# High and low rows side by side: one 512-column product in place of two of 256 columns, with the PSUM halves added afterwards

## The chip, the cores and the metric

The kernel runs on one core of a Trainium2 chip. The metric is the device time of one execution in microseconds (us). Every run is one launch with the same inputs.

## The reference

One layer of a hybrid diffusion backbone, batch 1, 256 latent tokens and 256 context tokens, model width 2048, float32. Two token mixers run in parallel, an RWKV-7 scan (branch a) and a gated DeltaNet (branch b). The change lies behind them, where the branches are merged, projected, and put through the feed-forward part:

```python
def gated_merge(o_a, o_b, gate_cols, p_a, p_b, w_out):
    g_a, g_b = jnp.split(gate_cols, 2, axis=-1)
    m = jax.nn.sigmoid(g_a) * (o_a @ p_a) + jax.nn.sigmoid(g_b) * (o_b @ p_b)
    return m @ w_out

def swiglu(h, w_gate_up, w_down):
    gate, up = jnp.split(h @ w_gate_up, 2, axis=-1)
    return (jax.nn.silu(gate) * up) @ w_down
...
        x = x + gt1 * y
        x = x + gt2 * swiglu(modulate(rmsnorm(x, norm2_w[layer]), sh2, sc2),
                             ffn_w_gate_up[layer], ffn_w_down[layer])
    return rmsnorm(x, final_norm_w)
```

`o_a` and `o_b` are 256 x 1024, `p_a` and `p_b` 1024 x 2048, `w_out` 2048 x 2048, gate and up together 2048 x 11264, down 5632 x 2048. The six modulation rows (`sh1` to `gt2`) come from one more product, of the condition vector with a 2048 x 12288 matrix.

## The kernel before

Everything is stored with channels on the 128 partitions and the 256 tokens along the free dimension (`T = 256`). A product with a weight matrix makes one tile of 128 output channels at a time and runs over the input channels in steps of 128 (`k`). Accuracy comes from a split into two numbers of the type float32r, one that TensorE takes in a single pass: a value is a high part (the value cast) plus a low part (the value less the high part). A step is then three products into the same 256 columns of a PSUM bank, in `gemm` (L376):

```python
E.matmul(ps, hi, Xh[:, k, :n], start=first and i == 0, stop=False)
E.matmul(ps, hi, Xl[:, k, :n], start=False, stop=False)
E.matmul(ps, lo, Xh[:, k, :n], start=False, stop=last and i == len(wt) - 1)
```

The weights arrive as float32 and are split on the chip, in `load_w`: a piece of eight steps (128 x 1024 numbers) is loaded into `wraw` on the SyncE queue, ScalarE casts it into `whi` (L370), VectorE subtracts into `wlo` (L371), and TensorE uses both. There are three buffers of `wraw` and two each of `whi` and `wlo` (four from the ninth tile of the first merge half to the end of the output projection). A cast can begin when TensorE has done with the piece that holds the buffer.

The stages behind the mixers, each a loop over output tiles `j`:

- First merge half: 16 tiles of 8 steps with the rows `Oa` (`oah`, `oal`), each multiplied by its sigmoid gate out of PSUM (L1589) into `PA`.
- Second merge half: 16 tiles of 8 steps with the rows of branch b in the same `Oa`, multiplied by the gate (L1609), added to `PA` (L1610), and split into the rows `M` (`mh`, `ml`).
- Output projection: 16 tiles of 16 steps with `M`. VectorE adds each, scaled, to the stream `x1` (L1623), ScalarE squares it, VectorE sums the squares (L1626). In these three loops VectorE also accumulates two modulation rows, the shift and scale of the feed-forward part, from a matrix that the GpSimd queue loads in 32 pieces: 31 steps on `acc` (L1565), one at each start of a row (L1567). For each row, four small matmuls sum over partitions, and a copy (`arow`, L1552), two transposes and two adds (L1557) bring it into `mod`. The tiles' first weights for gate and up (`w4`) are split in the same loop.
- Seam: sum of the squares by two pairs of matmuls with ones (L401), logarithm and exponential on ScalarE, and normalisation into the rows `Hf` (`hfh`, `hfl`, L1654 to L1656). It needs `x1` in full and `mod`.
- Gate and up: 44 pairs of tiles with 16 steps each. Gate and up share a bank, 256 columns each. ScalarE makes the SiLU out of PSUM (L1676), VectorE multiplies it with the up half out of PSUM (L1677), and the result is split into `Z` (`za` for the first 32 tiles, `zb` for the rest; L385, L386). The first two pairs use `w4`. In 32 of the tiles the last modulation row is made beside it (`aw`, L1688).
- Down: 16 tiles of 44 steps with `Z`, added to `x1` (L1701) as in the projection; then the last norm and the store.

The order of each engine's instructions in these stages is set when the program is built: a scheduler sorts what the code emits by its own estimate of times. Only what is wrapped in `tc.keep_in_program_order` keeps its place. On the chip each engine takes its instructions in that order. `pst` takes a PSUM bank from a pool: `pmm` has three (tile name `mm`), `psq` two (`s`).

Of the kernel before, what the change touches and what calls it, by code (L numbers as in the profile page):

```python
# [18 lines left out]
P = 128  # L19
D = 2048  # L20
KT = D // P
T = 256
# [261 lines left out]
def emit(ctx: ExitStack, tc, A, out, dbg=None):  # L284
# [91 lines left out]
    def gemm(ps, wt, X, n, first=True, last=True):  # L376

        Xh, Xl = X
        for i, (k, hi, lo) in enumerate(wt):
            E.matmul(ps, hi, Xh[:, k, :n], start=first and i == 0, stop=False)  # L380
            E.matmul(ps, hi, Xl[:, k, :n], start=False, stop=False)  # L381
            E.matmul(ps, lo, Xh[:, k, :n], start=False, stop=last and i == len(wt) - 1)  # L382

# [1193 lines left out]
    Oa = (gp.tile([P, 8, T], F32R, name="oah"), gp.tile([P, 8, T], F32R, name="oal"))  # L1577
    for i in range(0, 8, 2):
        split(Oa[0][:, i:i + 2, :], Oa[1][:, i:i + 2, :], rows[:, i:i + 2, :])
# [3 lines left out]
    for j in range(KT):  # L1583
# [16 lines left out]
    for i in range(0, 8, 2):  # L1600
        split(Oa[0][:, i:i + 2, :], Oa[1][:, i:i + 2, :], ob[:, i:i + 2, :])
    m_ctx = ExitStack()
    mp = m_ctx.enter_context(tc.tile_pool(name="mp", bufs=1, reuse_waits="tile"))
    M = (mp.tile([P, KT, T], F32R, name="mh"), mp.tile([P, KT, T], F32R, name="ml"))
    for j in range(KT):
        ps = pst(pmm, "mm")
        gemm(ps[:, 0:T], load_w(A["pb"][j], P, 8), Oa, T)
        m = x1p.tile([P, T], F32, tag="m", name="m")
        V.tensor_mul(m, ps[:, 0:T], gts[:, 16 + j])  # L1609
        V.tensor_add(m, m, PA[:, j])  # L1610
        split(M[0][:, j], M[1][:, j], m)
# [36 lines left out]
    with tc.tile_pool(name="fp", bufs=1, reuse_waits="tile") as fp:  # L1648
        Hf = (fp.tile([P, KT, T], F32R, name="hfh"), fp.tile([P, KT, T], F32R, name="hfl"))
        s2 = x1p.tile([P, 16], F32, name="s2")  # L1650
        V.scalar_tensor_tensor(s2, mod[:, 64:80], 1.0, p_("n2"), ALU.add, ALU.mult)
        for k in range(KT):
            hb = x1p.tile([P, T], F32, tag="hb", name="hb")
            V.scalar_tensor_tensor(hb, x1[:, k, :], s2[:, k:k + 1], r, ALU.mult, ALU.mult)  # L1654
            S.activation(Hf[0][:, k, :], hb, AF.Identity, bias=mod[:, 48 + k:49 + k])
            V.scalar_tensor_tensor(Hf[1][:, k, :], hb, mod[:, 48 + k:49 + k], Hf[0][:, k, :].bitcast(F32),  # L1656
                                   ALU.add, ALU.subtract)
        p4 = [pst(pmm, "mm") for _ in range(2)]
        for k in range(KT):
            for a in range(4):  # L1660

                gemm(p4[a // 2][:, T * (a % 2):T * (a % 2) + T], w4[a][k:k + 1], Hf, T,
                     k == 0 and a % 2 == 0, k == KT - 1 and a % 2 == 1)
        Z = (zap.tile([P, 2, 32, T], F32R, tag="za", name="za"), fp.tile([P, 2, NH - 32, T], F32R, name="zb"))
# [3 lines left out]
        for j in range(NH):  # L1668
            if j < 2:
                ps = p4[j]  # L1670
# [135 lines left out]
```

## Time and profile before

| what | value |
|---|---|
| median of 3 runs | 2228.19 us (2222.93 to 2228.29) |
| the profiled execution | 2235.21 us, its span 2233.3 us |
| granted TensorE clock, mean over the span | 0.983 |
| TensorE matmuls busy | 2158.9 us, 97% |
| VectorE, ScalarE busy | 1554.9 us (70%), 1062.6 us (48%) |
| first product of the merge, of gate and up, of down, from the span's start | 1268.9, 1470.9 and 1968.9 us |

How the lines are read: `L382 PE MATMUL mm<-hfh,wlo` is line 382, on TensorE, writing the tile `mm` from `hfh` and `wlo`. PE is TensorE's matmuls, PEld its weight loads, DVE is VectorE, ACT ScalarE, POOL GpSimd, SP SyncE. In groups, `x1344 | 376.3, 280 | 0.0` means 1344 instructions, 376.3 us busy, 280 ns each, and 0.0 us in which the engine sat idle before them, followed by who ended that wait. In a timeline a row is start, duration, engine, line and operation; `[1.52 <-PE mm L381]` is an idle time before it and what ended it. A table of windows has, per stretch of time, the busy time of each engine with its instructions, then the granted clock, the share of the DMA engines and GB/s.

### The profile page before, as it was taken

The page shows a single profiled execution, that of the slowest core. Times are in us where ns is not written, and L with a number is a line of the kernel's source. Part 1 is how long each engine was busy: PE and PEld are TensorE (multiplying, and loading weights), DVE is VectorE, ACT ScalarE, POOL GpSimd, SP SyncE. Part 2 cuts the span into 40 slices and gives each one's busy share as a digit, 9 for nine tenths or more (in the row PEclk, how much of TensorE's full clock was granted, in tenths as well). Part 3 has the DMA queues.
Part 4 walks back from the last instruction along what each step waited for, and adds up shares of the span by engine and source line. Part 5 has one row for each costly group of instructions (what it writes and reads, how often), then busy time and mean ns, then how long its engine had stood idle before and what let it go on. Part 6 is the DMA issues. An engine that isn't in the chain of part 4 may idle for free.

```text
span 2233.3 us, 54391 instructions
## 1 busy us (share of the span) xinstructions
PE 2158.9 (97%) x22780; PEld 1929.1 (86%) x22780; DVE 1554.9 (70%) x3244; ACT 1062.6 (48%) x1872; POOL 95.0 (4%) x171
## 2 busy tenths in 40 slices
PE   6998999999999999999999999999999999999998
PEld 4776687777778788878789999999999999999997
DVE  3457487788888668898998788955666565444444
ACT  3256545444554555544455555544444444444443
POOL 0000000000000011011110010100000000000000
PEclk9999899999999999999999999999999999999999
DMA  9975544344343446555567798937777776566665
GB/s 382 414 193 172 158 116 121 97 115 108 97 123 109 113 139 196 161 177 180 172 196 254 263 345 271 350 102 231 232 233 228 236 234 198 187 183 185 182 183 158
DMA packets 234484, 435.13 MB, mean 195 GB/s; under 512 B 115328, under 2 KB 129664, under 8 KB 229888
## 3 DMA queue, kind: packets, MB, share of 16 engines
q1 hardware_dynamic: 206304, 355.11, 50.6%
q0 software_dynamic: 14112, 51.39, 7.1%
q10 hardware_dynamic: 13824, 25.17, 3.4%
q8 instruction: 178, 2.92, 0.5%
q14 instruction: 66, 0.54, 0.1%
HBM read 405.76 MB, written 25.84 MB: 193 GB/s over the span
## 4 chain that ended last, share of the span: by engine, by line
PE 45%; issue 39%; DVE 9%; DMA 4%; ACT 2%; POOL 0%; SPq 0%; POOLq 0%; ACTq 0%; DVEq 0%
PE mm L147 22%; PE s L147 6%; PE pa L147 4%; DVE arena L147 3%; PE pi L147 3%; PE mm L380 3%; PE mm L382 2%; PE mm L381 2%; DVE wlo L147 2%; PE mm L477 1%; DVE aw L147 1%; DMA wraw<-w_low 1%; DMA aw<-ada_rest 1%; DMA ct<-ctxT 0%; DVE LAl L147 0%
## 5 line engine op out<-in xcount | busy, mean ns | idle before, releaser
L371 DVE TENSOR_TENSOR wlo<-wraw,whi 128x1024 fp32r<-128x1024 f32 x328 | 392.7, 1198 | 327.0 <-ACT whi L370 324.0
L370 ACT CAST whi<-wraw 128x1024 fp32r<-128x1024 f32 x328 | 336.6, 1028 | 467.7 <-PE mm L381 408.7
L147 PE MATMUL mm<-hxh,whi 128*128 128x256 f32 (+1 forms) x1376 | 466.1, 339 | 4.1 <-ACT whi L147 2.4
L147 PE MATMUL mm<-hxh,wlo 128*128 128x256 f32 (+1 forms) x1376 | 463.8, 337 | 5.0 <-DVE wlo L147 4.7
L147 PE MATMUL mm<-hxl,whi 128*128 128x256 f32 (+1 forms) x1376 | 463.3, 337 | 0.7 <-issue 0.7
L382 PE MATMUL mm<-hfh,wlo 128*128 128x256 f32 x1344 | 376.3, 280 | 0.0
L380 PE MATMUL mm<-hfh,whi 128*128 128x256 f32 x1344 | 375.1, 279 | 0.0
L381 PE MATMUL mm<-hfl,whi 128*128 128x256 f32 x1344 | 375.0, 279 | 0.0
L147 PEld LDWEIGHTS mm<-hxh,wlo 128*128 128x128 f32 x1376 | 265.1, 193 | 31.1 <-DVE wlo L147 7.8
L147 PEld LDWEIGHTS mm<-hxh,whi 128*128 128x128 f32 x1376 | 264.8, 192 | 28.2 <-ACT whi L147 3.2
L147 PEld LDWEIGHTS mm<-hxl,whi 128*128 128x128 f32 x1376 | 264.5, 192 | 23.5 <-issue 4.0
L147 DVE TENSOR_TENSOR wlo<-wraw,whi 128x512 fp32r<-128x512 f32 x344 | 236.9, 690 | 49.6 <-ACT whi L147 48.4
L381 PEld LDWEIGHTS mm<-hfl,whi 128*128 128x128 f32 x1344 | 252.5, 188 | 0.0
L382 PEld LDWEIGHTS mm<-hfh,wlo 128*128 128x128 f32 x1344 | 252.3, 188 | 0.2 <-DVE wlo L371 0.2
L380 PEld LDWEIGHTS mm<-hfh,whi 128*128 128x128 f32 x1344 | 251.4, 187 | 0.0
L147 ACT CAST whi<-wraw 128x512 fp32r<-128x512 f32 x344 | 205.5, 617 | 83.1 <-PE mm L147 57.3
L147 DVE TENSOR_TENSOR arena<-arena 128x28 f32<-128x28 f32 (+13 forms) x538 | 131.4, 246 | 23.0 <-DMA arena<-scr 10.0
L380 PE MATMUL mm<-za,whi 128*128 128x256 f32 x512 | 145.1, 283 | 0.0
L382 PE MATMUL mm<-za,wlo 128*128 128x256 f32 x512 | 145.0, 283 | 0.0
L381 PE MATMUL mm<-za,whi 128*128 128x256 f32 x512 | 144.9, 283 | 0.0
L147 ACT ACTIVATE arena<-arena 128x512 f32<-128x512 f32 (+3 forms) x132 | 76.6, 593 | 45.6 <-DVE arena L147 33.8
L380 PEld LDWEIGHTS mm<-za,whi 128*128 128x128 f32 x512 | 98.2, 192 | 0.0
(325 smaller groups left out, 3897.9 us busy)
## 6 DMA issues: line engine op xcount, KB each, us to landing
wraw<-w SPq DMA_DIRECT2D x172, 512.0 KB, 4.1
wraw<-wgu SPq DMA_DIRECT2D x168, 512.0 KB, 4.7
aw<-ada_rest POOLq DMA_DIRECT2D x96, 512.0 KB, 5.3
aw<-ada_first SPq DMA_DIRECT2D x32, 1024.0 KB, 12.6
wraw<-wdn SPq DMA_DIRECT2D x64, 448.0 KB, 3.5
wraw<-wout SPq DMA_DIRECT2D x32, 512.0 KB, 6.6
aw<-ada_gt ACTq DMA_DIRECT2D x64, 256.0 KB, 4.8
wraw<-wdn SPq DMA_DIRECT2D x32, 512.0 KB, 3.6
```

The lines of the kernel that those rows point to most:

```text
L147: return Op(self, cost, lambda: getattr(self.engine, name)(out, *a, **k), kind)
L370: S.copy(hi[:, c, :M], raw[:, c, :M])
L371: V.tensor_sub(lo[:, c, :M], raw[:, c, :M], hi[:, c, :M].bitcast(F32))
L380: E.matmul(ps, hi, Xh[:, k, :n], start=first and i == 0, stop=False)
L381: E.matmul(ps, hi, Xl[:, k, :n], start=False, stop=False)
L382: E.matmul(ps, lo, Xh[:, k, :n], start=False, stop=last and i == len(wt) - 1)
L477: E.matmul(ps[32 * g:32 * g + 32, 0:P], ckr[:, k].rearrange("p a b -> p (a b)"), aws[e, c][:, i, g], start=k == 0, stop=k == KT - 1)
```

## The change

The high and low rows of an operand become one tile with the two beside each other for every step (`[P, k, 2, T]`). In `gemm_wide` the high weights go once through both, 512 columns, and fill a whole bank: high times high in the left half, high times low in the right. The low weights go through the high rows and add to the right half. A step has two products in place of three, and the same 768 columns. The halves are added afterwards: `both` copies the right one with ScalarE and adds the left one with VectorE; where the result goes into `x1`, the update is made twice, once from each half. Gate and up take a bank each, up from the pool `psq`.

```diff
+    def gemm_wide(ps, wt, X, first=True, last=True):
+        for i, (k, hi, lo) in enumerate(wt):
+            E.matmul(ps, hi, X[:, k].rearrange("p a t -> p (a t)"), start=first and i == 0, stop=False)
+            E.matmul(ps[:, T:512], lo, X[:, k, 0], start=False, stop=last and i == len(wt) - 1)
+
+    def both(out, ps):
+        S.copy(out, ps[:, T:512])
+        V.tensor_add(out, ps[:, 0:T], out)
...
-    Oa = (gp.tile([P, 8, T], F32R, name="oah"), gp.tile([P, 8, T], F32R, name="oal"))
+    Oa = gp.tile([P, 8, 2, T], F32R, name="oa")
...
-        gemm(ps[:, 0:T], load_w(A["pa"][j], P, 8), Oa, T)
+        gemm_wide(ps, load_w(A["pa"][j], P, 8), Oa)
...
-        V.tensor_mul(PA[:, j], ps[:, 0:T], gts[:, j])
+        both(PA[:, j], ps)
+        V.tensor_mul(PA[:, j], PA[:, j], gts[:, j])
...
-        V.tensor_mul(m, ps[:, 0:T], gts[:, 16 + j])
+        both(m, ps)
+        V.tensor_mul(m, m, gts[:, 16 + j])
...
-        gemm(ps[:, 0:T], load_w(A["wout"][j], P, KT), M, T)
-        V.scalar_tensor_tensor(x1[:, j, :], ps[:, 0:T], mod[:, 32 + j:33 + j], x1[:, j, :], ALU.mult, ALU.add)
+        gemm_wide(ps, load_w(A["wout"][j], P, KT), M)
+        for part in (ps[:, T:512], ps[:, 0:T]):
+            V.scalar_tensor_tensor(x1[:, j, :], part, mod[:, 32 + j:33 + j], x1[:, j, :], ALU.mult, ALU.add)
...
-        p4 = [pst(pmm, "mm") for _ in range(2)]
+        p4 = [pst(pmm, "mm") if a % 2 == 0 else pst(psq, "s") for a in range(4)]
...
-                ps = pst(pmm, "mm")
-                gemm(ps[:, 0:T], load_w(A["wgu"][2 * j], P, KT), Hf, T)
-                gemm(ps[:, T:512], load_w(A["wgu"][2 * j + 1], P, KT), Hf, T)
+                pg, pu = pst(pmm, "mm"), pst(psq, "s")
+                gemm_wide(pg, load_w(A["wgu"][2 * j], P, KT), Hf)
+                gemm_wide(pu, load_w(A["wgu"][2 * j + 1], P, KT), Hf)
             g = fp.tile([P, T], F32, tag="g", name="g", bufs=2)
-            S.activation(g, ps[:, 0:T], AF.Silu)
-            V.tensor_mul(g, ps[:, T:512], g)
+            u = fp.tile([P, T], F32, tag="u", name="u", bufs=2)
+            both(g, pg)
+            S.activation(g, g, AF.Silu)
+            both(u, pu)
+            V.tensor_mul(g, u, g)
...
-                gemm(ps[:, 0:T], [(k - 32 * i, hi, lo) for k, hi, lo in wt if k // 32 == i],
-                     (z[:, 0], z[:, 1]), T, i == 0, i == 1)
-            V.scalar_tensor_tensor(x1[:, j, :], ps[:, 0:T], mod[:, 80 + j:81 + j], x1[:, j, :], ALU.mult, ALU.add)
+                gemm_wide(ps, [(k - 32 * i, hi, lo) for k, hi, lo in wt if k // 32 == i], z, i == 0, i == 1)
+            for part in (ps[:, T:512], ps[:, 0:T]):
+                V.scalar_tensor_tensor(x1[:, j, :], part, mod[:, 80 + j:81 + j], x1[:, j, :], ALU.mult, ALU.add)
```

The scheduler sorts the new instructions in, and moves others. Two places matter below. A line number of the changed kernel is 10 to 14 higher than before: the update L1623 is now L1636, L1565 (`acc`) L1575, L1552 (`arow`) L1562, L1557 (`mod`) L1567, L1626 (sum of squares) L1639.

VectorE at the end of the output projection, before the change. `arena<-mm` is the update of `x1` by an output tile, `acc` a step of a modulation row, `arow` and `mod` its end; the last update belongs to the last tile:

```order
L1565 SCALAR_TENSOR_TENSOR acc<-aw,ck,acc 128x1024
L1623 SCALAR_TENSOR_TENSOR arena<-mm,mod,arena 128x256
L371 TENSOR_TENSOR wlo<-wraw,whi 128x1024 x2
L1626 TENSOR_TENSOR arena<-arena 128x256
L371 TENSOR_TENSOR wlo<-wraw,whi 128x1024
L1552 COPY arow<-pa 128x256
L1623 SCALAR_TENSOR_TENSOR arena<-mm,mod,arena 128x256
L371 TENSOR_TENSOR wlo<-wraw,whi 128x1024
L1626 TENSOR_TENSOR arena<-arena 128x256
L1557 TENSOR_TENSOR mod<-pa,PR 128x4 x2
L1651 SCALAR_TENSOR_TENSOR arena<-mod,PR 128x16
L1623 SCALAR_TENSOR_TENSOR arena<-mm,mod,arena 128x256
```

The same end after the change:

```order
L371 TENSOR_TENSOR wlo<-wraw,whi 128x1024
L1575 SCALAR_TENSOR_TENSOR acc<-aw,ck,acc 128x1024
L1639 TENSOR_TENSOR arena<-arena 128x256
L1636 SCALAR_TENSOR_TENSOR arena<-mm,mod,arena 128x256 x2
L1575 SCALAR_TENSOR_TENSOR acc<-aw,ck,acc 128x1024
L1636 SCALAR_TENSOR_TENSOR arena<-mm,mod,arena 128x256
L1639 TENSOR_TENSOR arena<-arena 128x256
L1575 SCALAR_TENSOR_TENSOR acc<-aw,ck,acc 128x1024
L1562 COPY arow<-pa 128x256
L1567 TENSOR_TENSOR mod<-pa,PR 128x4 x2
L1664 SCALAR_TENSOR_TENSOR arena<-mod,PR 128x16
```

The last two steps of `acc` and the end of the row, which stood ahead of the last tile's update, now stand behind its first half; the second half stands between the two steps.

ScalarE in one pair of tiles of gate and up, before the change (`g<-mm` is the SiLU, `za<-g` the split's cast, `aw` a load that ScalarE's queue issues):

```order
L370 CAST whi<-wraw 128x1024 x2
L1676 ACTIVATE g<-mm 128x256
L370 CAST whi<-wraw 128x1024
L385 CAST za<-g 128x256
L370 CAST whi<-wraw 128x1024
L1687 DMA aw<-ada_gt 128x512 x2
```

And after it:

```order
L370 CAST whi<-wraw 128x1024
L391 COPY g<-mm 128x256
L1701 DMA aw<-ada_gt 128x512 x2
L370 CAST whi<-wraw 128x1024
L1689 ACTIVATE g<-g 128x256
L370 CAST whi<-wraw 128x1024
L391 COPY u<-s 128x256
L370 CAST whi<-wraw 128x1024
L395 CAST za<-g 128x256
```

Every one of the four casts of weights now has another instruction of ScalarE behind it, two of them copies out of PSUM, and the SiLU reads what VectorE has added (L392) in place of the bank.

More of the change, by code (lines that the diff above doesn't have):

```diff
@@ L1576, in emit @@
     PA = gp.tile([P, KT, T], F32, name="PA")
[L1577 removed]
+    Oa = gp.tile([P, 8, 2, T], F32R, name="oa")
     for i in range(0, 8, 2):
[L1579 removed]
+        split(Oa[:, i:i + 2, 0], Oa[:, i:i + 2, 1], rows[:, i:i + 2, :])
     gts = gp.tile([P, 32, T], F32, name="gts")
@@ L1648, in emit @@
     with tc.tile_pool(name="fp", bufs=1, reuse_waits="tile") as fp:
-        Hf = (fp.tile([P, KT, T], F32R, name="hfh"), fp.tile([P, KT, T], F32R, name="hfl"))
+        Hf = fp.tile([P, KT, 2, T], F32R, name="hf")
         s2 = x1p.tile([P, 16], F32, name="s2")
```

21 lines of the change are left out of this document (10 added, 11 removed).

## The prediction

> **What bounds the kernel now.** I read the head of the page first, then the costliest groups.
>
> ```profile
> span 2233.3 us, 54391 instructions
> PE 2158.9 (97%) x22780; PEld 1929.1 (86%) x22780; DVE 1554.9 (70%) x3244; ACT 1062.6 (48%) x1872; POOL 95.0 (4%) x171
> L371 DVE TENSOR_TENSOR wlo<-wraw,whi 128x1024 fp32r<-128x1024 f32 x328 | 392.7, 1198 | 327.0 <-ACT whi L370 324.0
> L370 ACT CAST whi<-wraw 128x1024 fp32r<-128x1024 f32 x328 | 336.6, 1028 | 467.7 <-PE mm L381 408.7
> L382 PE MATMUL mm<-hfh,wlo 128*128 128x256 f32 x1344 | 376.3, 280 | 0.0
> ```
>
> TensorE sits at 97%, and the wait columns run in a circle that ends there: the subtraction on VectorE (L371) waits for the cast on ScalarE (L370), and the cast waits for TensorE to give a weight buffer back. The products (L382) wait for nothing. That is the whole kernel, though, and the change touches only its last 950 us, so I asked for the stages of that stretch: end of the first merge half, second half, output projection, the seam before the feed-forward part, gate and up, down.
>
> ```profile
> core 0: us, PE busy (x) PEld busy (x) DVE busy (x) ACT busy (x) POOL busy (x), PEclk, DMA share, GB/s
> 1305.00:1328.00 23.00, 22.87 (x192) 22.86 (x192) 22.78 (x27) 15.97 (x21) 3.73 (x7) 1.00 0.98 357
> 1328.00:1374.00 46.00, 45.62 (x384) 45.43 (x383) 42.72 (x70) 22.73 (x32) 2.65 (x5) 1.00 0.79 279
> 1374.00:1467.00 93.00, 92.96 (x792) 91.50 (x791) 81.13 (x100) 47.20 (x57) 8.51 (x16) 1.00 0.90 317
> 1494.00:1969.00 475.00, 475.00 (x4033) 474.83 (x4032) 273.05 (x384) 202.32 (x255) 0.00 (x0) 1.00 0.69 218
> 1969.00:2222.00 253.00, 252.75 (x2115) 252.49 (x2113) 120.88 (x127) 107.05 (x128) 0.00 (x0) 1.00 0.61 178
> ```
>
> In the last two rows TensorE alone is full and VectorE idles for nearly half the time. In the first three VectorE is as full as TensorE: 22.78 of 23, 42.72 of 46, 81.13 of 93 us. A shorter product is therefore worth something in gate, up and down, and an added VectorE instruction costs something in the merge.
>
> **What a product costs.** A matmul's busy time (280 ns) overlaps the next one, so the price is the distance between starts. From the window rows it is 475.00 / 4033 = 117.8 ns in gate and up, and 252.75 / 2115 = 119.5 ns in down. A 512-column product of this kind occurs in the input projection, which the change leaves alone. The first and last starts of an undisturbed run of each width there:
>
> ```profile
> 825.63 0.39 PE L147 MATMUL mm<-hxh,whi 128*128 128x512 f32 x1
> ...
> 831.98 0.39 PE L147 MATMUL mm<-hxl,whi 128*128 128x512 f32 x1
> 1207.14 0.28 PE L147 MATMUL mm<-hxh,whi 128*128 128x256 f32 x1
> ...
> 1210.73 0.28 PE L147 MATMUL mm<-hxh,whi 128*128 128x256 f32 x1
> ```
>
> 28 steps in 6.35 us make 226.8 ns at 512 columns, 30 steps in 3.59 us make 119.7 at 256. The slope is 107.1 / 256 = 0.418 ns a column, and 12.6 ns are left that each instruction costs whatever its width. The changed group does the same columns (512 + 256 instead of three times 256) in one instruction fewer, so it saves that fixed part. With 107.1 ns of columns, the fixed part is 117.8 - 107.1 = 10.7 ns in gate and up, and 119.5 - 107.1 = 12.4 in down.
>
> - Gate and up: 88 tiles x 16 = 1408 steps x 10.7 ns = 15.1 us less.
> - Down: 16 tiles x 44 = 704 steps x 12.4 ns = 8.7 us less. Together 23.8.
>
> What no row shows is 512 and 256 columns in turn, all the time. Rows at a switch bound it, once up and once down, and so does a run of 512 just after an interruption:
>
> ```profile
> 841.49 0.28 PE L147 MATMUL mm<-hxh,wlo 128*128 128x256 f32 x1
> 841.61 0.40 PE L147 MATMUL mm<-hxh,whi 128*128 128x512 f32 x1
> 841.84 0.40 PE L147 MATMUL mm<-hxl,whi 128*128 128x512 f32 x1
> 852.29 0.39 PE L147 MATMUL mm<-hxh,wlo 128*128 128x512 f32 x1
> 852.52 0.28 PE L147 MATMUL mm<-hxh,whi 128*128 128x256 f32 x1
> 852.63 0.28 PE L147 MATMUL mm<-hxl,whi 128*128 128x256 f32 x1
> 766.09 0.40 PE L147 MATMUL mm<-hxh,wlo 128*128 128x512 f32 x1
> ...
> 768.18 0.39 PE L147 MATMUL mm<-hxh,wlo 128*128 128x512 f32 x1
> ```
>
> A pair takes 0.35 us at the first switch and 0.34 at the second. The disturbed run makes 9 steps in 2.09 us, 232 ns each, and so a pair of 352. Against three times 119.7 = 359 that saves from 7 to 19 ns a step. The undisturbed rows give 226.8 + 119.7 = 346.5, inside these ends, and I take them because gate, up and down run undisturbed. The ends move the 23.8 us to 12.0 (5.6 ns less on each of 2112 steps) and to 37.3 (6.4 ns more).
>
> The Trainium skill ("TensorE: Matmul & The Clock Gate", section "Back-to-back issue gap") puts the fixed part at about 2.5 ns. By that the two stages would save an estimated 2112 x 2.5 ns = 5.3 us, and the sum below would end at 2233. The rows above disagree with it (12.6 ns).
>
> **What the change adds.** Every output tile is put together from two PSUM halves: one ScalarE copy and one more VectorE add, or a second update (L1623, L1701) where the result goes into x1. Their spacing on VectorE, from two in a row, and the weight of the accumulation that they push aside:
>
> ```profile
> 1267.21 0.36 ACT L147 COPY arena<-mm 128x256 f32<-128x256 f32 x1
> 1335.23 0.75 DVE L1609 TENSOR_TENSOR arena<-mm,gts 128x256 f32<-128x256 f32 x2
> 1469.81 0.88 DVE L1654 SCALAR_TENSOR_TENSOR arena<-arena 128x256 f32<-128x256 f32 x2 [2.46 <-ACT arena L407]
> L1565 DVE SCALAR_TENSOR_TENSOR acc<-aw,ck,acc 128x1024 f32<-128x1024 f32 x30 | 38.4, 1279 | 0.0
> ```
>
> An add takes 0.75 - 0.42 = 0.33 us more of the queue, an update 0.88 - 0.48 = 0.40.
>
> *In gate and up* the additions are 44 x 2 of each kind: VectorE rises by 29 us from 273 in 475, ScalarE by 32 from 202. Work of that size is hidden by TensorE, as long as nothing comes late. Both queues keep their order, so I looked at how late a weight piece may be:
>
> ```profile
> 1601.21 0.28 PE L381 MATMUL mm<-hfl,whi 128*128 128x256 f32 x1
> 1601.57 1.05 ACT L370 CAST whi<-wraw 128x1024 fp32r<-128x1024 f32 x1 [1.52 <-PE mm L381]
> 1602.66 1.23 DVE L371 TENSOR_TENSOR wlo<-wraw,whi 128x1024 fp32r<-128x1024 f32 x1
> ```
>
> The last product that reads the old high piece starts at 1601.21. The cast follows at 1601.57, the subtraction ends at 1603.89. The piece between begins two products after that reader, at 1601.45, and lasts 24 x 0.118 = 2.83 us; the low half of the next one is first read two products into it, at 1604.51: 0.62 us to spare. Afterwards a piece is 8 x 10.7 = 86 ns shorter, so about 0.53 us remain. In the new order the copies of g and u stand between casts, and the SiLU (L1689) waits for an add that has one subtraction ahead of it; but a cast waits 1.5 us for TensorE before it starts, and the extra 0.36 us of a copy fit into that. I take no cost here, and 0 as the lower end.
>
> *At the entry of gate and up* four banks are emptied at once while the first streamed pieces are made: 4 x 0.36 + 4 x 0.33 = 2.8 us if none is hidden, nothing if all is. I take 1.5.
>
> *In the merge* VectorE becomes the bound. From 1305 to 1467 (162 us) it is busy for 22.78 + 42.72 + 81.13 = 146.6 us. It gets 24 adds (192 products in the first row are 8 tiles, and the second half has 16) x 0.33 and 16 updates x 0.40, 14.3 us: 160.9. TensorE needs 448 steps x 12 ns = 5.4 us less than now, 156.6. Ends: 5.4 us less where the adds find idle time, 14.3 more where every old wait stays. Most of VectorE's 15.4 idle us are waits that vanish when it runs late; those for data that comes late itself stay, such as
>
> ```profile
> DVE w L1639 <- ACT w L1638: 4.1, 3, 2.0
> ```
>
> (total, times, longest). 160.9 + 4.1 = 165.0, so 3.0 us longer.
>
> *At the seam* into the feed-forward part the accumulation of the modulation row (L1565) gave way to the adds: two of its steps and the sum over them now stand behind the last output tile's first update (the order shown above). Before, the sum ran during the projection:
>
> ```profile
> 1457.80 0.64 PE L1550 MATMUL pa<-acc,C 128*32 128x256 f32 x8
> 1466.67 0.59 PE L401 MATMUL pa<-arena,C 128*128 128x256 f32 x2
> 1468.12 0.70 PE L401 MATMUL pa<-arena,C 128*128 128x256 f32 x2 [0.85 <-ACT arena L413]
> 1470.89 0.51 PE L380 MATMUL mm<-hfh,w 128*128 128x256 f32 x2 [2.08 <-ACT hfh L1655]
> 192.00:203.00 11.00, 8.48 (x98) 7.70 (x100) 10.78 (x23) 8.28 (x17) 1.46 (x4) 0.84 0.40 117
> 1466.00:1474.00 8.00, 5.07 (x36) 4.16 (x36) 4.31 (x11) 3.12 (x7) 0.00 (x0) 1.00 0.32 106
> ```
>
> To it come the second update (0.40), two accumulations (2 x 1.20 spaced), the sum's matmuls (0.64) and about 0.5 for its copy and adds beside the logarithm and exponential: 3.9 us. The last row shows the clock at 1.00 across today's gaps of 0.85 and 2.08 us; the row above it, from an early stage where TensorE was busy for 8.48 of 11 us, has 0.84: 11 x 0.16 = 1.8 us lost. With gaps 4 us wider I count half of that, 0.9. So 4.8 us, between 0.4 (the accumulations catch up) and 8.
>
> The Trainium skill (same page, "Why this matters for your kernels") asks for no TensorE gap over some 3 us, else the clock falls back; by that the 1.8 would be due in full, and the sum 0.9 us higher. Today's gaps, all under it, agree.
>
> *At the end* the last tile gets its second update, 0.40 us that nothing hides.
>
> **The sum.** -23.8 + 0 + 1.5 + 3.0 + 4.8 + 0.4 = -14.1 us. The profiled execution took 2235.2 us with a span of 2233.3; the median of the three runs shown is 7.0 lower, 2228.2, and I set the sum against that: 2214.1.
>
> **The rivals.**
>
> - *The alternation never settles.* Every 512-column product pays what the disturbed run shows: gate, up and down save 12.0 us instead of 23.8, and the time is 2226, no change to be measured. For it: each pair holds a switch. Against it: the two switches sum to 0.69 us for two pairs, as the undisturbed rows do. The Trainium skill's 2.5 ns (section named above) would be the far end of this rival, 2233; the rows leave that 0.02 of its 0.13.
> - *Slower: the queues of gate and up come late.* The place is the low half of a weight piece. The copies, the SiLU and the split now make ScalarE wait for VectorE and VectorE for ScalarE once more in each of the 44 tiles. The gain is gone, and 6.7 us beyond it, when TensorE loses (14.1 + 6.7) / 44 = 0.47 us a tile, that is, when one piece in each tile is about 1 us later than now. Against it: the cast still waits 408.7 us for TensorE in all. At 0.55 us a tile the time is 2238.
> - *The merge costs nothing.* The adds fit into idle time and the accumulations end before the seam: 2228.2 - 23.8 - 5.4 + 0.4 + 1.5 + 0.4 = 2201. Against it: 160.9 us of work for 156.6.
>
> **How the numbers follow.** About 0.3%, 6.7 us, is what a measurement of this kernel can tell from no change. The forecast has 0.67 (its own range is 2206 to 2223), the unsettled alternation 0.13, late queues 0.13, the free merge 0.07. The range 2203 to 2229 leaves out the late queues and some of the free merge. Faster: nearly all of the forecast and the free merge, 0.71; the same: the alternation and the forecast's edge, 0.16; slower: 0.13.
>
> **What would show it.** Right: in gate and up a 512-column start to the next start at 224 to 227 ns and the 256 after it at 117 to 120, PE full, some 460 us for what takes 475; down at about 244; VectorE over 95% from 1305 to the end of the projection, with waits of TensorE for wlo there, and accumulations behind the last tile. Wrong: PE gaps in front of wlo in every tile of gate and up, or a pair at 352 ns and more.

## The result, and the profile after

The changed kernel takes 2249.39 us (median of 4 runs, 2246.05 to 2251.91), the kernel before 2228.24 beside it. The recorded ratio is 1.0081, with a 95% interval of 1.0058 to 1.0104; the two medians alone would give 1.0095. The forecast was 2214.1 us. The change makes the kernel slower, by about 18 us (21 by the medians), and the time lies outside the forecast's range.

The two profiled executions lie 13.1 us apart in span (2246.4 and 2233.3 us), since that of before was itself 7 us above its median. By stages, from the first product of one to the first of the next in the two traces (the seam and the end begin where the last product of the projection and of down ends), in us:

| stage | before | after | difference | forecast |
|---|---|---|---|---|
| two merge halves | 105.1 | 119.7 | +14.6 | +3.0 with the next |
| output projection | 92.8 | 92.8 | 0.0 | |
| seam | 4.1 | 9.1 | +5.0 | +4.8 |
| first four tiles (two pairs) of gate and up | 22.9 | 25.2 | +2.3 | -0.7 |
| the other 84 | 475.1 | 475.1 | 0.0 | -14.4, entry +1.5 |
| down | 252.8 | 247.0 | -5.8 | -8.7 |
| end | 11.6 | 12.1 | +0.5 | +0.4 |

The differences sum to 16.6; the remaining -3.5 lies ahead of the merge, in code that the change leaves alone.

The same stages in the windows of the changed kernel (merge, projection, seam, first four tiles; then the rest of gate and up, down). The columns are those of the windows in the prediction.

```profile
1265.40:1385.10 119.70, 104.47 (x573) 89.46 (x572) 93.69 (x161) 66.83 (x111) 8.74 (x16) 0.94 0.78 272
1385.10:1477.90 92.80, 91.83 (x524) 78.76 (x522) 85.31 (x112) 47.39 (x58) 9.01 (x17) 1.00 0.91 317
1477.90:1486.90 9.00, 2.94 (x14) 1.65 (x14) 5.82 (x13) 2.21 (x5) 0.00 (x0) 0.74 0.15 44
1486.90:1512.10 25.20, 25.18 (x128) 21.83 (x129) 12.11 (x29) 6.49 (x15) 0.00 (x0) 0.89 0.05 17
...
1512.00:1987.20 475.20, 473.03 (x2690) 412.56 (x2689) 305.61 (x471) 229.14 (x343) 0.00 (x0) 1.00 0.68 218
1987.20:2234.30 247.10, 247.08 (x1412) 215.56 (x1410) 126.91 (x142) 108.83 (x128) 0.00 (x0) 1.00 0.62 182
```

Three things are to be seen. In the merge TensorE is idle for 15.2 of 119.7 us, and yet VectorE is not full either (93.69): both wait. The clock is below 1.00 in the merge, the seam and the first tiles. And in the rest of gate and up TensorE is full (473.03 of 475.2 us), with a third fewer products than before (2690 for 4033), and the time is the same.

**The merge.** TensorE's longest wait there, with what VectorE and GpSimd did ahead of it (timelines: start, duration, in brackets idle time and what ended it):

```profile
1331.34 0.53 POOL L1573 DMA_DIRECT2D aw<-ada_rest  x1 [4.61 <-DVE acc L1575]
1332.32 2.60 DVE L1575 SCALAR_TENSOR_TENSOR acc<-aw,ck,acc 128x1024 f32<-128x1024 f32 x2
1339.35 1.28 DVE L1575 SCALAR_TENSOR_TENSOR acc<-aw,ck,acc 128x1024 f32<-128x1024 f32 x1 [4.43 <-DMA aw<-ada_rest]
1340.55 1.22 DVE L371 TENSOR_TENSOR wlo<-wraw,whi 128x1024 fp32r<-128x1024 f32 x1
1341.69 0.42 DVE L392 TENSOR_TENSOR arena<-mm,arena 128x256 f32<-128x256 f32 x1
...
1334.88 0.28 PE L388 MATMUL mm<-oa,wlo 128*128 128x256 f32 x1
1342.16 0.80 PE L387 MATMUL mm<-oa,whi 128*128 128x512 f32 x1 [7.00 <-DVE arena L392]
```

TensorE needs a bank, and the bank needs the add (L392). VectorE takes its instructions in order, and ahead of the add stand three accumulation steps. The third one's block was only ordered at 1331.34, when an earlier step gave its buffer back, and VectorE stands 4.43 us until it lands. Before, the same steps started at 1331.70, 1334.03 and 1338.50, with other work between them. The loss of the merge is made here: up to the tile ahead of this wait the changed kernel is at most 1.6 us behind, counted from its first merge product; it is 8.6 behind with the product at 1342.16 and 14.8 three tiles later.

A wait costs a second time, by the clock. A short gap of TensorE earlier in the merge, in the timeline:

```profile
1301.38 0.50 PE L387 MATMUL mm<-oa,whi 128*128 128x512 f32 x1 [0.33 <-ACT whi L370]
1303.97 0.38 PE L388 MATMUL mm<-oa,wlo 128*128 128x256 f32 x1 [2.09 <-DVE wlo L371]
```

The windows behind this gap, behind the long one, and behind a third of 2.75 us:

```profile
1304.80:1308.20 3.40, 3.40 (x13) 2.92 (x12) 3.40 (x4) 3.40 (x6) 0.53 (x1) 0.50 0.90 306
1338.90:1345.70 6.80, 3.54 (x11) 3.06 (x12) 6.35 (x10) 0.00 (x0) 0.53 (x1) 0.50 0.60 204
1352.60:1356.00 3.40, 3.40 (x11) 2.88 (x11) 3.04 (x10) 1.11 (x3) 0.00 (x0) 0.50 0.49 159
```

13.6 us of the merge run at a granted clock of 0.50. TensorE was busy for 10.3 of them, so I estimate the clock's part of the 14.6 at half of that, about 5 us.

**The seam.** The two accumulation steps and the second update run behind the last tile, as the order had said, and TensorE waits 3.69 us:

```profile
1478.30 1.28 DVE L1575 SCALAR_TENSOR_TENSOR acc<-aw,ck,acc 128x1024 f32<-128x1024 f32 x1
1479.49 0.48 DVE L1636 SCALAR_TENSOR_TENSOR arena<-mm,mod,arena 128x256 f32<-128x256 f32 x1
...
1480.22 1.28 DVE L1575 SCALAR_TENSOR_TENSOR acc<-aw,ck,acc 128x1024 f32<-128x1024 f32 x1
...
1481.55 0.64 PE L1560 MATMUL pa<-acc,C 128*32 128x256 f32 x8 [3.69 <-DVE acc L1575]
...
1486.92 0.79 PE L387 MATMUL mm<-hf,w 128*128 128x512 f32 x1 [2.44 <-DVE hf L1669]
```

**Gate and up.** Two undisturbed stretches of the changed kernel (windows):

```profile
1525.00:1725.00 200.00, 200.00 (x1149) 175.18 (x1148) 135.33 (x216) 95.76 (x143) 0.00 (x0) 1.00 0.73 233
1740.00:1980.00 240.00, 240.00 (x1360) 209.24 (x1359) 150.87 (x227) 113.71 (x170) 0.00 (x0) 1.00 0.67 212
```

TensorE's starts at the place between them where the pace changes (timeline):

```profile
1731.57 0.39 PE L387 MATMUL mm<-hf,whi 128*128 128x512 f32 x1
...
1732.61 0.39 PE L387 MATMUL s<-hf,whi 128*128 128x512 f32 x1
1733.00 0.39 PE L388 MATMUL s<-hf,wlo 128*128 128x256 f32 x1
1733.22 0.39 PE L387 MATMUL s<-hf,whi 128*128 128x512 f32 x1
...
1734.26 0.40 PE L387 MATMUL s<-hf,whi 128*128 128x512 f32 x1
...
1735.32 0.40 PE L387 MATMUL s<-hf,whi 128*128 128x512 f32 x1
```

A pair is one product of 512 and one of 256 columns: 200 us / (1149 / 2) is 348 ns a pair in the first stretch, 240 / (1360 / 2) 353 in the second (the counts take in the product at each edge; by the starts it is 348.9 and 353.3). Three pairs take 1.04 us ahead of the break, 1.04 in the first three behind it, then 1.06. The break is one product that came 0.16 us late (0.39 instead of 0.23 to the next start) and its successor 0.11 late; its weights came late, since the cast of their piece had waited 2.16 us for a load. From there to the end of gate and up the slower pace stays. Before, three products took 3 x 117.8 = 353 ns.

### The profile page after: what moved, and what is told of

It reads as the page before. It is cut to its first block, busy times and chain, and to the rows that moved or that the text cites. A ratio compares the mean times of both kernels' runs of the same rounds, so it can differ in the third digit from the quotient of the medians.

```text
span 2246.4 us, 49451 instructions
## 1 busy us (share of the span) xinstructions
PE 2153.4 (96%) x20156; PEld 1803.2 (80%) x20156; DVE 1611.1 (72%) x3396; ACT 1098.8 (49%) x1992; POOL 93.4 (4%) x171
## 4 chain that ended last, share of the span: by engine, by line
issue 41%; PE 40%; DVE 9%; DMA 7%; ACT 2%; POOL 1%; SPq 0%; POOLq 0%; ACTq 0%; DVEq 0%
PE mm L147 20%; PE s L147 5%; PE pa L147 4%; PE mm L387 3%; DVE arena L147 3%; PE pi L147 2%; DMA aw<-ada_rest 2%; DVE wlo L147 2%; PE mm L388 2%; PE mm L487 1%; DVE aw L147 1%; DMA wraw<-w_low 1%; DMA wraw<-pa 1%; DMA scr<-arena 1%; DVE LAl L147 1%
## 5 line engine op out<-in xcount | busy, mean ns | idle before, releaser
L147 PEld LDWEIGHTS mm<-hxl,whi 128*128 128x128 f32 x1376 | 263.2, 191 | 23.8 <-issue 4.4
L387 PE MATMUL s<-hf,whi 128*128 128x512 f32 x672 | 238.1, 395 | 1.4 <-ACT whi L370 1.4
L387 PE MATMUL mm<-hf,whi 128*128 128x512 f32 x672 | 238.2, 395 | 0.0
L388 PE MATMUL s<-hf,wlo 128*128 128x256 f32 x672 | 189.2, 281 | 0.8 <-DVE wlo L371 0.8
L388 PE MATMUL mm<-hf,wlo 128*128 128x256 f32 x672 | 189.1, 281 | 0.0
L387 PE MATMUL mm<-za,whi 128*128 128x512 f32 x512 | 179.8, 395 | 0.0
L387 PEld LDWEIGHTS s<-hf,whi 128*128 128x128 f32 x672 | 126.4, 188 | 31.4 <-ACT whi L370 1.7
L387 PEld LDWEIGHTS mm<-hf,whi 128*128 128x128 f32 x672 | 126.5, 188 | 29.9
L388 PEld LDWEIGHTS s<-hf,wlo 128*128 128x128 f32 x672 | 126.0, 188 | 1.4 <-DVE wlo L371 1.4
L388 PEld LDWEIGHTS mm<-hf,wlo 128*128 128x128 f32 x672 | 126.2, 188 | 0.0
```

What stands on the lines that cost most here:

```text
L147: return Op(self, cost, lambda: getattr(self.engine, name)(out, *a, **k), kind)
L387: E.matmul(ps, hi, X[:, k].rearrange("p a t -> p (a t)"), start=first and i == 0, stop=False)
L388: E.matmul(ps[:, T:512], lo, X[:, k, 0], start=False, stop=last and i == len(wt) - 1)
```

## The experiments

The shares of the loss come from the time between the first merge product and the first of the last 84 tiles (column "merge to gate"), from these 84 tiles ("gate and up") and from down, all read in the profiled executions. The ratios are to runs of the kernel before on the same chip.

| kernel | ratio, 95% interval | merge to gate | gate and up | down |
|---|---|---|---|---|
| before | | 224.8 | 475.1 | 252.8 |
| changed | 1.0081 (1.0058 to 1.0104) | 246.7 | 475.1 | 247.0 |
| ff_only | 1.0000 (0.9984 to 1.0016) | 225.9 | 479.0 | 247.5 |
| half | 1.0009 (0.9993 to 1.0025) | 227.4 | 477.8 | 247.1 |
| no_acc | 1.0036 (1.0022 to 1.0050) | 233.6 | 477.3 | 247.7 |
| acc_resident | 1.0055 (1.0035 to 1.0075) | 238.5 | 474.5 | 247.4 |
| warm | 1.0092 (1.0074 to 1.0110) | 247.8 | 473.2 | 247.5 |
| grouped | 0.9984 (0.9968 to 0.9999) | 238.4 | 463.1 | 246.5 |
| ff_grouped | 0.9930 (0.9908 to 0.9952) | 226.1 | 463.5 | 246.5 |
| ff_grouped_al | 0.9937 (0.9919 to 0.9954) | 224.1 | 464.3 | 245.7 |
| ff_pairs | 0.9961 (0.9940 to 0.9983) | 225.8 | 465.2 | 245.8 |
| low_first | 0.9995 (0.9977 to 1.0014) | 227.9 | 477.6 | 247.1 |
| narrow | 0.9982 (0.9959 to 1.0006) | 225.8 | 474.9 | 252.8 |
| best | 0.9928 (0.9907 to 0.9950) | 225.2 | 463.1 | 246.5 |

**ff_only: gate, up and down alone.** Merge and projection are those of before:

```diff
-        gemm_wide(ps, load_w(A["pa"][j], P, 8), Oa)
+        gemm(ps[:, 0:T], load_w(A["pa"][j], P, 8), Oa, T)
...
-        both(PA[:, j], ps)
-        V.tensor_mul(PA[:, j], PA[:, j], gts[:, j])
+        V.tensor_mul(PA[:, j], ps[:, 0:T], gts[:, j])
...
-        for part in (ps[:, T:512], ps[:, 0:T]):
-            V.scalar_tensor_tensor(x1[:, j, :], part, mod[:, 32 + j:33 + j], x1[:, j, :], ALU.mult, ALU.add)
+        V.scalar_tensor_tensor(x1[:, j, :], ps[:, 0:T], mod[:, 32 + j:33 + j], x1[:, j, :], ALU.mult, ALU.add)
```

> Gate, up and down in the new form, merge and output projection as before. In the changed kernel the stretch from the first merge half to the first gate product is 18.6 us later than before, gate and up take 474.4 us (474.6 before) and down 246.9 (252.7). Theory 1, the loss lies in the merge, the projection and the gap behind them, and the new form gains little in gate and up because a pair of 512 and 256 columns takes 353 ns: about 2225 us (down 5.8 less, 1 to 3 more at the entry of gate and up). Theory 2, the loss comes from the feed-forward part (copies and adds there, four banks at the entry): 2235 to 2245.

2230.45 us, as before (2230.21). The whole loss is gone, so it lies in the merge, the projection and the seam (225.9 us there, against 246.7); the time is 5 over the first theory's. Gate and up ran at 353 ns a pair from the start (2 x 178 us / 1009):

```profile
1522.00:1700.00 178.00, 178.00 (x1009) 155.09 (x1009) 118.44 (x188) 84.32 (x127) 0.00 (x0) 1.00 0.73 234
```

**half, no_acc, acc_resident: what fills the merge.** `half` reads one half of each bank and leaves out the copies, the adds and the second updates (the diff shows the first merge half; the second and the projection likewise). `no_acc` leaves out the 30 accumulation steps on `acc` (15 behind the start of each row) and their loads, `acc_resident` the loads alone but for one block a row:

```diff
# half
-        both(PA[:, j], ps)
-        V.tensor_mul(PA[:, j], PA[:, j], gts[:, j])
+        V.tensor_mul(PA[:, j], ps[:, 0:T], gts[:, j])
# no_acc
-                if k:
-                    tc.keep_in_program_order(V.scalar_tensor_tensor(acc, w, ck[:, k, 0:1], acc, ALU.mult, ALU.add))
# acc_resident
-            for k in range(KT):
-                w = adp.tile([P, 1024], F32, tag="aw", name="aw", bufs=3)
-                G.dma_start(w, A["ada_rest"][b, :, k, :])
+            w = adp.tile([P, 1024], F32, tag="aw", name="aw", bufs=3)
+            G.dma_start(w, A["ada_rest"][b, :, 0, :])
+            for k in range(KT):
```

> The changed kernel, but merge and projection read only the first half of each bank (the product of the low parts is left out of the result): no copy, no extra add, no second update, the products themselves unchanged. Theory 1, the added instructions of VectorE make the loss: the stretch from the first merge product to the first of gate and up takes 224 to 229 us, the time is 2223 to 2230. Theory 2, the 512-column products at their place (the low weights needed sooner, pairs of 353 ns) make it: 238 to 247 us, the time 2240 to 2249.

> The changed kernel without the 30 accumulation steps (about 38 us of VectorE) of the two modulation rows, so these rows are not computed; the sums over them stay. From the first merge product to the first product of gate and up: before 225.5 us, changed 247.6, with the accumulations reading a resident block 239.3. Theory 1, VectorE has no room for adds and accumulations at once: 226 to 231 us, the stalls on arena and oa and the 4.0 us gap behind the projection are gone, the time is 2226 to 2233. Theory 2, the longer way from a full bank to an empty one (copy, then add, then product with the gate) holds TensorE by itself: 236 to 242 us, the time 2236 to 2243.

> The changed kernel, but the accumulation of the modulation row reads one resident block 32 times instead of streaming 32 blocks (so two modulation rows are not computed): VectorE has the same instructions, the stream is gone. Theory 1, the 7.3 us stall of TensorE in the second merge half is VectorE standing in front of an accumulation whose block lands late, with the adds that empty the banks queued behind it: the stall goes, with it one stretch of half clock (6.8 us at 0.5), 2236 to 2241. Theory 2, VectorE simply has too much work there: the stall stays within 2 us, 2246 to 2250.

The merge halves of the three in this order (windows):

```profile
1260.10:1366.30 106.20, 100.90 (x573) 86.70 (x572) 84.80 (x133) 58.05 (x79) 9.26 (x17) 0.98 0.86 306
```

```profile
1260.70:1370.50 109.80, 102.60 (x583) 87.13 (x582) 80.40 (x150) 65.62 (x108) 1.86 (x3) 0.98 0.68 233
```

```profile
1263.60:1376.90 113.30, 102.83 (x574) 87.99 (x572) 93.19 (x161) 65.90 (x109) 1.86 (x3) 0.97 0.67 224
```

The waits for a bank around the place of the 7.00 us, in `no_acc` and then in `acc_resident` (timeline of TensorE):

```profile
1337.29 0.47 PE L387 MATMUL mm<-oa,whi 128*128 128x512 f32 x1 [2.75 <-DVE arena L392]
```

```profile
1335.58 0.50 PE L387 MATMUL mm<-oa,whi 128*128 128x512 f32 x1 [1.21 <-DVE arena L392]
...
1344.23 0.47 PE L387 MATMUL mm<-oa,whi 128*128 128x512 f32 x1 [2.75 <-DVE arena L392]
```

Without the adds the stretch is 227.4 us and the time that of before, though the products are the new ones: the first theory of `half` holds, the form of the products costs the merge nothing to speak of, and the loss comes from what was added behind them. With the loads gone and every VectorE instruction kept, the 7.00 us are 1.21, the merge is 6.4 us shorter (119.7 to 113.3), and the stretch 8.2: the late block was that wait. It is not that the weights arrive sooner without the loads: in the merge ScalarE's casts wait 6.1 us for them in the changed kernel and 7.2 in `acc_resident`. The time (2243.3 us) lies between the two theories; the wait of 2.75 us is still there. `no_acc` has a stretch between its theories (233.6 us) and a time at the edge of the second (2236.6): TensorE still waits 1.21 and 2.75 us for adds at the same two tiles, with VectorE busy for only 80.40 of 109.8 us. There the copy stands on ScalarE behind the cast of a weight piece, and the add on VectorE behind its subtraction (at the second wait cast at 1334.51, copies at 1335.46, subtraction at 1335.59, adds at 1336.73). So the longer way from a full bank to an empty one holds TensorE by itself, for 6.2 us of the stretch (233.6 to 227.4); the accumulation's work beside it is another 4.9 (238.5 to 233.6), its late loads 8.2. Each share contains the half clock that its waits brought (3.4 us of the merge in `half` and `no_acc`, 6.8 in `acc_resident`, 13.6 in the changed kernel), and the order into which the scheduler sorts each kernel anew. These are single executions; the stretch of the kernels with the old merge alone varies from 224.1 to 227.9.

**warm: products that keep TensorE busy in the seam.**

```diff
+    warm = pst(psq, "s")
+    for _ in range(16):
+        tc.keep_in_program_order(E.matmul(warm, W4[:, 0, 0, 0], W4[:, 0, 0, 0:4].rearrange("p k t -> p (k t)"), start=True, stop=True))
     r = rms_scale(x1p, [ssum, sq], T, "rs")
+    for _ in range(12):
+        tc.keep_in_program_order(E.matmul(warm, ...))
```

> The changed kernel with 16 products of 512 columns into a spare bank behind the last projection tile and 12 more behind the sum over the squares, where TensorE stands for 3.7 and 2.9 us: the waits stay, TensorE is busy in them. Theory 1, the half clock after these gaps costs time: the clock stays at 1.00 from 1478 on, the first products of gate and up take 23.2 to 23.6 us instead of 26.1, the time is 2 to 3 us less, 2246 to 2247. Theory 2, the half clock falls into the gaps and costs nothing more: 2249 to 2250.

```profile
1474.60:1485.20 10.60, 8.34 (x44) 6.04 (x42) 5.84 (x13) 2.22 (x5) 0.00 (x0) 1.00 0.23 74
1485.20:1488.60 3.40, 3.40 (x11) 2.97 (x12) 3.04 (x8) 1.68 (x4) 0.00 (x0) 0.55 0.00 0
1485.20:1509.20 24.00, 24.00 (x129) 20.97 (x130) 12.07 (x29) 6.36 (x14) 0.00 (x0) 0.93 0.00 1
```

2249.15 us, no gain. The clock stayed up across the first gap, the first four tiles took 24.0 us instead of 25.2, and the seam itself grew from 9.1 to 10.6, as the real matmuls queue behind the added ones. One stretch of half clock, 3.4 us, was left behind the second gap, where TensorE still waits 2.23 us. So the second theory has the time, but not the reason: the half clock does cost time, and what filling the first gap won behind the seam (1.2 us) it lost in it. The stretch that stayed is worth another 1.7 us (half of 3.4, an estimate).

**grouped, ff_grouped: the products of a piece sorted by width.** In `gemm_wide`, over the steps of one weight piece (`part`):

```diff
-        for i, (k, hi, lo) in enumerate(wt):
-            E.matmul(ps, hi, X[:, k].rearrange("p a t -> p (a t)"), ...)
-            E.matmul(ps[:, T:512], lo, X[:, k, 0], ...)
+            for k, hi, lo in part:
+                E.matmul(ps, hi, X[:, k].rearrange("p a t -> p (a t)"), ...)
+            for k, hi, lo in part:
+                E.matmul(ps[:, T:512], lo, X[:, k, 0], ...)
```

> As the kernel with gate, up and down alone, and in each weight piece all 512-column products of the high weights first and then all 256-column products of the low ones: two switches of width a piece instead of sixteen. Theory A, the switch of width costs the missing 7 ns a pair: 512 columns step at 224 to 227 ns inside a group, gate and up take about 466 us, down about 240, the time is about 2210. Theory B, 512 columns of this operand cost 231 to 237 ns whatever stands beside them: 2225, as without the grouping.

> The changed kernel whole, with the products of a weight piece grouped by width. Theory A (the switch costs): gate, up and down about 14 us less, and the merge, where the low piece is then needed some 1.8 us later, loses less too: 2228 to 2236. Theory B (the operand costs): 2245 to 2250, at most the merge a little shorter.

Gate and up of `ff_grouped` in a window:

```profile
1490.00:1950.00 460.00, 459.88 (x2668) 404.73 (x2667) 302.38 (x467) 227.93 (x337) 0.00 (x0) 1.00 0.70 225
```

Three pieces in the timeline, where eight products stand in a row:

```profile
1699.69 1.99 PE L393 MATMUL mm<-hf,whi 128*128 128x512 f32 x8
1701.51 1.11 PE L396 MATMUL mm<-hf,wlo 128*128 128x256 f32 x8
1702.46 2.00 PE L393 MATMUL s<-hf,whi 128*128 128x512 f32 x8
1704.29 1.07 PE L396 MATMUL s<-hf,wlo 128*128 128x256 f32 x8
1705.20 1.07 PE L393 MATMUL s<-hf,whi 128*128 128x512 f32 x4
```

A pair takes 460 us / (2668 / 2) = 345 ns, and the rows show how: 512 columns in 1.82 / 8 and 1.83 / 8, 228 and 229 ns; 256 columns in 0.95 / 8 = 119 in one piece and 0.91 / 8 = 114 in the next. Gate and up take 463.5 us, and the kernel 0.9930 of before. Theory A holds in gate and up, though the steps of 512 columns are 225 to 232 ns, not 224 to 227. It does not hold in down, which went to 246.5 and not 240. `grouped`, at 2226.8 us, is about 1% faster than the changed kernel (1.0081 to 0.9984) and a little under what A gave: 12 us come from gate and up, 8.3 from the stretch ahead. There the low piece is needed later; TensorE's waits for low weights in the merge (2.8 us) are gone and those for a bank fell from 9.7 to 3.6 us, but no run separates the two.

**ff_pairs, low_first, ff_grouped_al, narrow: why the pace depends on the order.** Groups of two in place of eight; the low products into the other half of the bank; a pad of 64 bytes ahead of `za`; and the kernel before, its three products of 256 columns sorted by weights:

```diff
# ff_pairs: the key that forms a group
+            itertools.groupby(wt, lambda s: (piece_of.get(id(s[2])), s[0] // 2))
# low_first
-            E.matmul(ps[:, T:512], lo, X[:, k, 0], start=False, stop=last and i == len(wt) - 1)
+            E.matmul(ps[:, 0:T], lo, X[:, k, 0], start=False, stop=last and i == len(wt) - 1)
# ff_grouped_al
+    pad = ent(tc.tile_pool(name="zpad", bufs=1, side="right"))
+    pad.tile([P, 16], F32, name="zpad")
# narrow, in gemm
+            for k, hi, lo in part:
+                E.matmul(ps, hi, Xh[:, k, :n], ...)
+                E.matmul(ps, hi, Xl[:, k, :n], ...)
+            for k, hi, lo in part:
+                E.matmul(ps, lo, Xh[:, k, :n], ...)
```

> As the grouped kernel of gate, up and down, but in groups of two: two products of 512 columns, then two of 256. Alternating takes 353.3 ns a pair (16 switches in 8 pairs), groups of eight 344.6 (2 switches). Theory 1, each switch up and down costs the same: 69.6 / 7 = 9.9 ns each, with four in 8 pairs 344.6 + 3 x 9.9 / 8 = 348.3 ns a pair, gate and up 468 us, the time 2221. Theory 2, the sequence locks into a fixed pattern of steps and the count of switches does not matter by itself: 353 ns and 475 us (2228), or 345 ns and 463 us (2216), not between.

> Gate, up and down alone in the new form, 512 and 256 columns in turn, but the products of the low weights add to the first half of the bank instead of the second (both halves are added in the end). Theory 1, a product of 256 columns that adds to the columns which the product of 512 has just written makes the pair slow: with the first half 345 to 347 ns a pair, gate and up 464 to 467 us, the time 2216 to 2219. Theory 2, the half has no part in it, the alternation by itself locks into 349 or 353 ns a pair: gate and up 469 to 478 us, the time 2224 to 2231.

> Gate, up and down in the new form with the products grouped by width, and a pad of 64 bytes ahead of the larger operand of down (za), so that its rows start at a multiple of 128 bytes like those of gate and up. Theory 1, the start of a row is why za runs at 230.6 and 118.7 ns where gate and up run at 228.9 and 115.7: za goes to 345 ns a pair, down from 246.5 to about 244 us, the time is 2 to 2.5 us under the grouped one, 2213.5. Theory 2, the address has no part in it: 2216, down 246.5.

> The kernel before, all products 256 columns wide, but in each weight piece the products of the high weights first (high and low rows in turn), then those of the low weights; nothing is added afterwards. Theory 1, the grouped kernel is faster because it has one instruction less in each step: 117.7 ns a product as before, gate and up 475 us, down 253, the time 2226 to 2228. Theory 2, it is faster because of the order: products of 256 columns at 113 to 116 ns, gate and up 460 to 467 us, the time 2215 to 2220.

Gate and up of `ff_pairs`, `low_first` and `narrow`; then down of `ff_grouped` and of `ff_grouped_al` (windows):

```profile
1497.00:1709.00 212.00, 212.00 (x1228) 186.08 (x1227) 143.28 (x228) 104.71 (x158) 0.00 (x0) 1.00 0.71 231
```

```profile
1550.00:1960.00 410.00, 410.00 (x2323) 356.83 (x2321) 264.05 (x406) 194.31 (x290) 0.00 (x0) 1.00 0.66 222
```

```profile
1490.00:1963.00 473.00, 473.00 (x4019) 473.00 (x4017) 272.32 (x382) 201.66 (x252) 0.00 (x0) 1.00 0.68 219
```

```profile
1951.00:2196.00 245.00, 245.00 (x1402) 215.05 (x1401) 125.49 (x142) 106.24 (x127) 0.00 (x0) 1.00 0.62 183
```

```profile
1956.00:2200.00 244.00, 244.00 (x1401) 213.10 (x1401) 125.44 (x142) 106.22 (x127) 0.00 (x0) 1.00 0.62 184
```

Groups of two run at 2 x 212 us / 1228 = 345 ns, like groups of eight, with four times the switches: theory 1 falls, a switch has no price of its own, and the second theory holds for the pace. The time, 2221.3 us, is that of theory 1; its interval overlaps that of `ff_grouped`. `low_first` stays at 2 x 410 / 2323 = 353 ns: which half the low products add to has no part in it. The pad gives 348 ns a pair in down for 349 without it (244 and 245 us for 1401 and 1402 products), so the start of a row is not the reason either, or a small one. `narrow` stays at 473 / 4019 = 117.7 ns: sorting alone brings nothing, the one instruction less is needed too.

**best: also the low weights last in the old merge.** `ff_grouped` with the `gemm` of `narrow`.

> Gate, up and down in the new form and grouped by width; merge and projection in the old form, but with the low weights of a piece at the end of its products, so that they are needed 1.9 us later. In the grouped kernel TensorE still waits 1.0, 1.8 and 1.1 us for low weights and rows in the first merge half. If these waits go, 2.8 us less than the grouped kernel (2216): 2213. If others take their place, 2216.

2216.39 us, 0.9928 of before, no different from `ff_grouped`: the second alternative. TensorE's waits for low weights in the merge (3.0 us in all in `ff_grouped`) went, waits for high pieces came (4.0 in all, 2.0 the longest). Both kernels beat the one before and the changed one.

## Why the prediction was wrong

- **The price of a pair (-23.8, measured -8.0).** This step failed most. Of the 8.0 us, 5.8 are down's; the last 84 tiles of gate and up give 2.2, since their 0.0 contains 2.2 us of waits at the entry (below). What the first four tiles save, 0.7 by the forecast, is hidden by the clock. The forecast took 226.8 ns for 512 columns from a run of equal products and 119.7 for the 256 after it. In turn, a pair runs at 349 or 353 ns in gate and up. The rows of the prediction held the answer, and they were read against the wrong base: the pairs of 340 to 353 ns at switches and in the disturbed run were set against 3 x 119.7 = 359, the pace of other operands, while three products of gate and up took 353. Even the 346.5 that the prediction settled on is only 7 ns under that, where its sum took 10.7. Set against 353, a pair of 352 saves 1.4 ns a step there and 6.5 in down, 6.6 us in all, and the rival in which the alternation never settles would have stood at 2231 instead of 2226. The end of 12.0 us was too kind for the same reason. That rival described what happened in gate and up; it got 0.13.
- **The fixed part exists, but is smaller than worked out.** Sorted by width, the pair is 345 ns in gate and up, 8.4 under three old products, where the forecast had 10.7; in down it is 349, 9 under them, where it had 12.4. So `ff_grouped` takes 0.9930 of the time, and even it gets 17.9 us out of these two stages (11.6 and 6.3) of 23.1. The Trainium skill ("TensorE: Matmul & The Clock Gate", section "Back-to-back issue gap") would give, by its formula for isolated products, an estimated 512 / 2.4 + 256 / 2.4 + 2 x 2.5 = 325 ns for a pair; 345 is the least that any run here shows over a stage.
- **Gate and up hide the adds (0): right.** TensorE is busy for 200.00 of 200 us in a steady stretch. The rival of late queues did not come.
- **Entry of gate and up (+1.5, 0 to 2.8): right in size, +2.2.** Two waits in a row, for a high and a low piece:

```profile
1519.35 0.49 PE L387 MATMUL s<-hf,whi 128*128 128x512 f32 x1 [1.40 <-ACT whi L370]
1520.61 0.39 PE L388 MATMUL s<-hf,wlo 128*128 128x256 f32 x1 [0.77 <-DVE wlo L371]
```

- **Merge (+3.0, measured +14.6).** The step that failed is the sum over the stretch: VectorE's work against TensorE's, as if each could run whenever it liked. The projection did come out even. In the merge neither engine is full: VectorE waits for a block, TensorE for VectorE, and then the clock halves. VectorE was to be over 95% busy, with TensorE waiting for low weights; it was 78% in the merge and 92% in the projection, and TensorE waited for a bank. What the loads, the accumulation and the longer way each take stands under the experiments. The upper end of the range, 14.3, was reached by other causes than those it was made from.
- **Seam (+4.8, measured +5.0): right**, with the accumulations behind the last tile, but the clock in it (0.9) was sized too low. It is 0.50 for 10.2 us from 1482.3 on, 5.6 of them in the first four tiles, which lose about 2.8 us by it (half of 5.6, an estimate) on top of the 5.0. That is most of what those tiles missed (+2.3 for -0.7). Not all of it is the change's: `ff_only`, with old merge and old seam, has 24.2 us there, and `narrow`, with the old products alone, 24.4, for 22.9 in the profile of before.
- **Clock.** The prediction weighed the Trainium skill's bound (same page, "Why this matters for your kernels": no TensorE gap over some 3 us) and found today's gaps under it. The waits of 7.00 and 3.69 us agree with the bound. The wait of 2.75 us and the gap ahead of 1303.97, 2.09 us with 0.33 just before it, are under it and were each followed by 3.4 us at 0.50, while 0.85 and 2.08 us in the seam of before were not. The traces say why. In each of the 14, the stretches of half clock start whole multiples of 3.413 us apart; the three in the merge of the changed kernel and the one at its seam lie 10, 4 and 38 of them from one to the next. I cut the time from 1250 to 1500 us into the windows of that grid. At full clock, a window with at most 1.60 us of idle TensorE was never followed by half clock (954 windows), one with 1.91 us or more always was (31), and in the 8 between both happened. The gap of 2.08 us in before falls on a border of the grid, with 1.32 and 1.61 us of idle time in the two windows; one of 2.07 us in the seam of `narrow` lies in one window, and the clock halves.
- **End (+0.4): right**, +0.5.

## What to carry to other kernels

Fewer and wider products only pay at the pace at which they run in the new sequence; the price of a step has to be compared with the same operands' old step, and here mixed widths ran best in groups (345 ns a pair in gate and up against 349 to 353 in turn). Where an engine is close to full, the sum of its work says little: look for instructions in its queue that wait for a load, and ask what stands behind them. A bank that is emptied in two instructions on two engines instead of one is held longer, and TensorE can wait for it even where VectorE has time to spare; more banks might help, which no run here tried. A wait of two or three microseconds on TensorE can cost again as half clock, and whether it does can change from one kernel to the next with the place where the gap falls.

## What the hardware showed that was not expected

- TensorE's steps settle into a repeating pattern, and the same sequence of instructions has more than one: 349 and 353 ns a pair with the widths in turn. In the changed kernel the pace went from the first to the second where one product came 0.16 us late, and it stayed for the remaining 250 us. `half` goes the other way too, by the starts of its products from 353 ns a pair before 1580 us to 349 around 1620, and back. Two eights of 256 columns in neighbouring pieces run at 119 and 114 ns. The count of switches, the half of the bank and (all but 1 ns) the start of a row are not what sets it; what does stays open.
- A granted clock of 0.50 lasted 3.4, 6.8 or, behind the seam, 10.2 us: one, two or three windows of the grid above. In the merge it begins 3 to 4 us after the start of the gap, in two of the three cases over products that are running again. About half a window of idle time can be enough, and the position of a gap on the grid decides.
